# The first norm of a two-layer block: both row tiles of a quarter ahead of the next quarter's modulation copy, and the shift's small operations ahead of the normalised tiles

## The chip, the cores and the metric

The kernel runs on one core of one Trainium2 chip. The metric is the device time of one launch, in microseconds (us). The core has five engines that run side by side, each through its own instructions in order: PE multiplies (its weight loads are shown as PEld), DVE and ACT work on whole tiles element by element, POOL does a little of the same and issues some transfers, SP issues most transfers. A tile lies in on-chip memory on 128 partitions; PE writes its results to eight accumulator banks (PSUM), which DVE and ACT read.

## The reference, cut to what matters

Two layers of a diffusion block over 256 tokens of `x` and 256 of a context `h_ctx`, 1024 wide. Each layer has two gated feed-forward halves around a middle with three branches (neighbourhood attention, window attention, convolution), each behind a normalisation whose scale and shift are products of a conditioning vector. The change touches only the start of the first feed-forward half of the first layer:

```
for l in range(DEPTH):
    mx = split(silu(c) @ w_ada[l] + b_ada[l], 9)       # mx[0] shift, mx[1] scale, mx[2] gate, ...
    mc = split(silu(c_ctx) @ w_ada[l] + b_ada[l], 9)   # the same for the context
    x = x + 0.5*mx[2]*swiglu(rms_norm(x, g[l,0])*(1 + mx[1]) + mx[0], w_ffn1_gu[l], w_ffn1_down[l])
    h_ctx = ...                                        # the same with mc
    ...                                                # middle, second feed-forward half
return rms_norm(x, final_g)

swiglu(h, w_gu, w_down): a, b = split(h @ w_gu); return (silu(a)*b) @ w_down
```

## The kernel before, in words

Activations lie transposed: eight row tiles `R[k]` of 128 features by 512 columns (256 of `x`, then 256 of the context). Every product in full precision is made of three matmuls at reduced precision (`mm3`, L327, L328, L329): high part of the weights by high and by low part of the data, low part by high part. The two parts are made by a split: ACT rounds the value to the high part (L123), DVE subtracts (L124). For weights these are `wh` and `wl`, made from a raw block `raw` that SP's queue brings in (L280); `weights(k)` does it for row tile `k` of the first four weight columns. Four raw buffers form a ring; later in the program the rows of the conditioning's weights (`araw` at L246) go through the same ring.

The opening is `FirstNorm.blocks`. It starts four of the feed-forward's first columns before the norm's root is known: it multiplies the weights by `R[k]` scaled by `modA` (1 + scale, times the norm's weight), and only at the end applies the root `rs` and adds the shift's part. It runs in four quarters `q` of two row tiles each:

- `ada_first(1, q)` makes the scale for the quarter, in two steps of a generator that `go` advances. The first step is 32 small matmuls (L208, into `ada`) and a copy by DVE (L213, `adas`); the second is a transposing matmul (L216, `adat`) and DVE's `mod` (L219), `modt` (L176) and `modA` (L178).
- `scale(k)` makes the two parts of the scaled tile, in two halves each: `qh` on ACT (L521), `ql` on DVE (L522).
- `prod(k)` is 4 columns by 3 matmuls into the four banks `f`.
- `square(k)` is ACT's square (L389) and DVE's sum (L396), for the root.

Behind the quarters comes the shift. The same `ada_first` with chunk 0 makes it (`z[0]` to `z[3]`); `inv_rms` makes `rs` (L370); `parts_of(h)` splits half of the shift (`bb`), `product_of(h)` multiplies it by the four columns' weights (32 matmuls `fb`, L615), `rows_of` copies the row out (`br`, L622) and `fc` (L652) adds the two rows up. For the columns that follow, the normal way is used: `normed(k)` makes `nt` (L469), `hidden` adds the shift and splits into `Hh` (ACT, L494) and `Hl` (DVE, L495). The last two of the eight tiles are normed by POOL (L483), with ACT (L485) and a split. Then the columns `g` run, 8 tiles by 3 matmuls each.

When the feed-forward's first columns are out, `Ada.enter` starts the conditioning for the rest of the block: DVE copies one value into the tile `phase` (L236), POOL issues a transfer of 1 MB into it (L237), ACT takes SiLU of it (L238), and DVE then reduces one row of weights after the other against it (L250). DVE's `fs` (L659) and the gate's products (L725, L727, L730) follow.

The order of the instructions in the opening is the order in which the code is written: `in_order` pins it for each engine from the start of the blocks to `self.end`, and holds the 300 instructions that follow behind them. Behind `self.end`, a scheduler orders them as their inputs allow.

## Time and profile before

| | |
|---|---|
| median of 3 runs | 1979.52 us (1979.29 to 1980.55) |
| profiled execution | 1982.47 us |
| its span | 1980.7 us |
| granted PE clock, mean | 0.994 |
| PE busy | 1947.2 us, 98% of the span |
| DVE / ACT / POOL busy | 71% / 45% / 5% |

The span is the time from the first to the last instruction of the profiled execution. In a row of the timeline stand the start in us, the length, the engine, the line, the operation, the output and its inputs, and how many are taken together; in brackets the idle time before it and what ended it, as far as semaphores show it. A matmul's length is longer than its step: the next one starts before it ends.

### The profile page before, as it was taken

How to read it: one execution, taken by the hardware profiler on the slowest of the kernel's cores; microseconds unless marked ns; L12 is line 12 of the kernel's file. 1: busy time of each engine (PE TensorE's matmuls, PEld its weight loads, DVE VectorE, ACT ScalarE, POOL GpSimd, SP SyncE). 2: the span in 40 equal slices, each digit the busy share in tenths (PEclk: the TensorE clock that was granted, in tenths of full speed). 3: DMA queues.
4: the chain of work that ended last, by engine and by line, in shares of the span. 5: the costliest groups of instructions: out<-in, count | busy, mean ns of one | idle time of the engine just before them, and what ended most of it. 6: DMA issues, size and time to landing. Idle time of an engine off the chain costs nothing.

```text
span 1980.7 us, 29367 instructions
## 1 busy us (share of the span) xinstructions
PE 1947.2 (98%) x10760; PEld 1655.7 (84%) x10760; DVE 1400.4 (71%) x3203; ACT 898.3 (45%) x1765; POOL 106.2 (5%) x100
## 2 busy tenths in 40 slices
PE   6899999999999999999999999999999999999998
PEld 4788888888788888988888888888888988999998
DVE  3698677759867645876666669766665797787654
ACT  3433232344667744533232245323223567866553
POOL 0100000100011101100000010000001001020000
PEclk9899999999999999999999999999999999999999
DMA  8265545523221222354454535444554243355552
GB/s 303 86 227 185 173 152 178 185 76 120 84 75 55 94 97 96 107 172 159 158 160 159 170 107 170 156 154 154 166 170 134 93 146 124 128 179 182 183 185 103
DMA packets 82657, 287.40 MB, mean 145 GB/s; under 512 B 9296, under 2 KB 11088, under 8 KB 82128
## 3 DMA queue, kind: packets, MB, share of 16 engines
q1 hardware_dynamic: 79488, 277.91, 42.9%
q0 software_dynamic: 864, 4.98, 0.6%
q10 hardware_dynamic: 2160, 2.64, 0.5%
q8 instruction: 84, 1.38, 0.3%
q14 instruction: 61, 0.50, 0.1%
HBM read 284.44 MB, written 1.05 MB: 144 GB/s over the span
## 4 chain that ended last, share of the span: by engine, by line
PE 94%; DVE 2%; issue 1%; ACT 1%; DMA 1%; POOL 0%; SPq 0%; ACTq 0%; DVEq 0%; POOLq 0%
PE g L329 13%; PE g L328 13%; PE g L327 13%; PE pr L328 8%; PE pr L327 8%; PE pr L329 8%; PE b L327 4%; PE b L328 4%; PE b L329 4%; PE f L328 3%; PE f L329 3%; PE f L327 3%; PE sc L1050 1%; PE pv L1130 1%; PE pt L1111 1%
## 5 line engine op out<-in xcount | busy, mean ns | idle before, releaser
L123 ACT ACTIVATE wh<-raw 128x512 fp32r<-128x512 f32 x760 | 464.4, 627 | 567.8 <-PE g L328 177.7
L124 DVE TENSOR_TENSOR wl<-raw,wh 128x512 fp32r<-128x512 f32 x760 | 521.6, 696 | 162.1 <-ACT wh L123 157.5
L250 DVE CUSTOM_DVE_ANT_0 junk<-araw,phase 128x512 f32<-128x512 f32 x512 | 353.9, 691 | 235.6 <-DMA araw<-in_adaT_dram 221.7
L329 PE MATMUL g<-Hh,wl 128*128 128x512 f32 (+1 forms) x1240 | 457.8, 369 | 0.0
L327 PE MATMUL g<-Hh,wh 128*128 128x512 f32 (+1 forms) x1240 | 455.2, 367 | 1.8 <-ACT Hh L123 1.8
L328 PE MATMUL g<-Hl,wh 128*128 128x512 f32 (+1 forms) x1240 | 456.8, 369 | 0.0
L327 PEld LDWEIGHTS g<-Hh,wh 128*128 128x128 f32 x1240 | 233.7, 189 | 44.0 <-ACT Hh L123 2.3
L328 PEld LDWEIGHTS g<-Hl,wh 128*128 128x128 f32 x1240 | 234.1, 189 | 42.9 <-DVE Hl L124 0.2
L329 PEld LDWEIGHTS g<-Hh,wl 128*128 128x128 f32 x1240 | 233.6, 188 | 41.3 <-DVE wl L124 0.2
L328 PE MATMUL pr<-gl,wh 128*128 128x512 f32 (+1 forms) x704 | 258.0, 366 | 0.0
L327 PE MATMUL pr<-gh,wh 128*128 128x512 f32 (+1 forms) x704 | 258.0, 366 | 0.0
L329 PE MATMUL pr<-gh,wl 128*128 128x512 f32 (+1 forms) x704 | 257.5, 366 | 0.0
L327 PE MATMUL b<-Hh,wh 128*128 128x512 f32 (+1 forms) x480 | 167.1, 348 | 3.2 <-DVE rot L941 3.2
L328 PE MATMUL b<-Hl,wh 128*128 128x512 f32 (+1 forms) x480 | 163.9, 342 | 0.0
L329 PE MATMUL b<-Hh,wl 128*128 128x512 f32 (+1 forms) x480 | 163.9, 342 | 0.0
L327 PEld LDWEIGHTS pr<-gh,wh 128*128 128x128 f32 x704 | 132.4, 188 | 23.5
L328 PEld LDWEIGHTS pr<-gl,wh 128*128 128x128 f32 x704 | 132.5, 188 | 23.0
L329 PEld LDWEIGHTS pr<-gh,wl 128*128 128x128 f32 x704 | 132.4, 188 | 22.9
L123 ACT ACTIVATE gh<-g 128x512 fp32r<-128x512 f32 (+1 forms) x88 | 50.7, 576 | 218.3 <-DVE g L727 210.1
L328 PE MATMUL f<-ql,wh 128*128 128x258 f32 (+1 forms) x408 | 120.8, 296 | 7.4 <-DVE ql L522 7.4
L327 PE MATMUL f<-qh,wh 128*128 128x258 f32 (+1 forms) x408 | 124.0, 304 | 1.9 <-ACT qh L521 1.6
L329 PE MATMUL f<-qh,wl 128*128 128x258 f32 (+1 forms) x408 | 119.9, 294 | 0.0
(247 smaller groups left out, 2602.6 us busy)
## 6 DMA issues: line engine op xcount, KB each, us to landing
raw<-in_ws_dram SPq DMA_DIRECT2D x380, 512.0 KB, 3.5
araw<-in_adaT_dram SPq DMA_DIRECT2D x128, 512.0 KB, 4.1
araw<-in_ada_dram SPq DMA_DIRECT2D x32, 256.0 KB, 5.7
phase<-in_crow_dram POOLq DMA_DIRECT2D x3, 1024.0 KB, 8.3
tb<-in_rpb_dram ACTq DMA_DIRECT2D x12, 192.0 KB, 2.8
R<-in_xT_dram SPq DMA_DIRECT2D x8, 256.0 KB, 6.0
phase<-in_const_dram POOLq DMA_DIRECT2D x2, 640.0 KB, 6.2
out_dram<-fin SPq DMA_DIRECT2D x4, 256.0 KB, 3.3
```

What stands on the lines that cost most here:

```text
L123: nc.scalar.activation(out=hi, in_=src, func=AF.Copy)
L124: nc.vector.tensor_tensor(out=lo, in0=src, in1=f32(hi), op=ALU.subtract)
L250: nc.vector.tensor_tensor_reduce(out=junk, in0=raw[:, c], in1=self.rows[:, s, c], scale=1.0, scalar=0.0, op0=ALU.mult, op1=ALU.add, accum_ ...
L327: nc.tensor.matmul(ps, wh, xh, start=start, stop=False)
L328: nc.tensor.matmul(ps, wh, xl, start=False, stop=False)
L329: nc.tensor.matmul(ps, wl, xh, start=False, stop=stop)
L1050: nc.tensor.matmul(pss[s][:, o], a[r, c], b[r, k], start=i == 0, stop=i == 2)
L1111: nc.tensor.transpose(pt[:, n * P:(n + 1) * P], self.pf[v][s][:, o + i * P:o + (i + 1) * P], ident)
L1130: nc.tensor.matmul(self.po[s][:, sl], V[t0 + i][j // 2][:, c:c + P], p[:, k], start=m == 0, stop=m == n - 1)
```

## The change

Both halves of the change move code; no instruction is added or taken away. In the quarters, the odd tile's `weights` and `scale` and both squares stand ahead of the first `go(a)` of the next quarter (its matmuls and copy). Three matmuls (one column) of the odd tile stand between that and the second `go(a)`, and nine behind it. `weights(0)` is put between the first quarter's two steps. In the part on the shift, three normed tiles come first, then both remaining modulation groups, the first `fb`, both second steps and the second half's split; only then the early weights, and the other tiles. `hidden` runs for tiles 0 and 1, then 2, then 3 to 5.

```diff
             go(a)
+            weights(0)
             go(a)
             for q in range(4):
                 k = 2 * q
...
-                weights(k)
                 self.scale(k)
+                weights(k + 1)
                 prod(k)
-                if q < 3:
-                    a = ada_first(1, q + 1, raws[q + 1])
-                    go(a)
-                weights(k + 1)
                 self.scale(k + 1)
+                self.square(k, nc.vector)
+                self.square(k + 1, nc.vector)
                 if q == 3:
                     break
-                prod(k + 1, range(2))
+
+                a = ada_first(1, q + 1, raws[q + 1])
                 go(a)
-                prod(k + 1, range(2, n))
-                self.square(k, nc.vector)
-                self.square(k + 1, nc.vector)
+                prod(k + 1, [0])
+                weights(k + 2)
+                go(a)
+                prod(k + 1, range(1, n))
             zero = [ada_load(0, q) for q in range(4)]
             W.load()
             W.load()
-            self.square(KD - 2, nc.vector)
-            self.square(KD - 1, nc.vector)
             norm = inv_rms([self.sq], self.nq, oneD, res)
+            z = [ada_first(0, q, raws) for q, raws in enumerate(zero)]
             prod(KD - 1, [0, 1])
-            z = [ada_first(0, q, raws) for q, raws in enumerate(zero)]
...
             self.rs = res[0]
-            self.H, nts = [], []
+            self.H = []
             prod(KD - 1, [3])
-            go(z[2])
-            product_of(0)
-            nts += [self.normed(k) for k in (0, 1)]
+            nts = [self.normed(k) for k in range(3)]
             go(z[2])
             go(z[3])
-            rows_of(0)
-            nts += [self.normed(k) for k in (2, 3)]
-            self.hidden(range(2), nts)
+            pb = product_of(0)
+            go(z[2])
             go(z[3])
             parts_of(1)
-            product_of(1)
-            self.hidden(range(2, 4), nts)
-            nts += [self.normed(k) for k in range(4, KD - N_POOL)]
-            rows_of(1)
-            self.hidden(range(4, KD - N_POOL), nts)
+            rows_of(pb)
+            pb = product_of(1)
             for _ in range(N_EARLY):
                 W.make()
+            self.hidden(range(2), nts)
+            rows_of(pb)
+            self.hidden([2], nts)
+            nts += [self.normed(k) for k in range(3, KD - N_POOL)]
+            self.hidden(range(3, KD - N_POOL), nts)
             self.end = traced()
             self.hidden(range(KD - N_POOL, KD))
```

`product_of` now returns its bank and `rows_of` takes it. Lines behind the middle of this part stand two lines higher in the new file (L615 becomes L614, L652 becomes L650, L655 becomes L653, L725 becomes L723).

DVE in the second quarter, before (tile 2's `ql` first; `wl` and `ql` behind `adas` are those of the odd tile 3):

```order
L522 SCALAR_TENSOR_TENSOR ql_267<-R_81,modA_104,qh_266 128x256 x2
L213 COPY adas_301<-ada_284 128x128
L124 TENSOR_TENSOR wl_304<-raw_135,wh_303 128x512
L522 SCALAR_TENSOR_TENSOR ql_308<-R_82,modA_104,qh_307 128x256 x2
L219 TENSOR_TENSOR mod_103<-adat_319,vt 128x4
L176 TENSOR_SCALAR modt_322<-mod_103 128x4
L178 TENSOR_TENSOR modA_104<-modt_322,vt 128x4
L396 TENSOR_TENSOR sq_245<-sq_245,sq_331 128x512
L396 TENSOR_TENSOR sq_245<-sq_245,sq_334 128x512
L124 TENSOR_TENSOR wl_338<-raw_172,wh_337 128x512
L522 SCALAR_TENSOR_TENSOR ql_342<-R_83,modA_104,qh_341 128x256 x2
```

and the same piece now:

```order
L522 SCALAR_TENSOR_TENSOR ql_267<-R_81,modA_104,qh_266 128x256 x2
L124 TENSOR_TENSOR wl_273<-raw_135,wh_272 128x512
L522 SCALAR_TENSOR_TENSOR ql_289<-R_82,modA_104,qh_288 128x256 x2
L396 TENSOR_TENSOR sq_208<-sq_208,sq_294 128x512
L396 TENSOR_TENSOR sq_208<-sq_208,sq_297 128x512
L213 COPY adas_317<-ada_300 128x128
L124 TENSOR_TENSOR wl_323<-raw_176,wh_322 128x512
L219 TENSOR_TENSOR mod_103<-adat_326,vt 128x4
L176 TENSOR_SCALAR modt_329<-mod_103 128x4
L178 TENSOR_TENSOR modA_104<-modt_329,vt 128x4
L522 SCALAR_TENSOR_TENSOR ql_342<-R_83,modA_104,qh_341 128x256 x2
```

The odd tile's `wl` and `ql` and both sums of squares went ahead of the copy `adas`; behind it stands the next quarter's `wl`.

DVE in the part on the shift, before, from the copy of `z[2]` to the second half's `bb`:

```order
L213 COPY adas_579<-ada_562 128x128
L469 SCALAR_TENSOR_TENSOR nt_614<-R_79,modA_104,rs_557 128x256 x2
L469 SCALAR_TENSOR_TENSOR nt_617<-R_80,modA_104,rs_557 128x256 x2
L219 TENSOR_TENSOR mod_103<-adat_620,vt 128x4
L213 COPY adas_640<-ada_623 128x128
L622 COPY br_642<-fb_581 4x512
L469 SCALAR_TENSOR_TENSOR nt_644<-R_81,modA_104,rs_557 128x256 x2
L469 SCALAR_TENSOR_TENSOR nt_647<-R_82,modA_104,rs_557 128x256 x2
L495 SCALAR_TENSOR_TENSOR Hl_651<-nt_614,mod_103,Hh_650 128x256 x2
L495 SCALAR_TENSOR_TENSOR Hl_657<-nt_617,mod_103,Hh_656 128x256 x2
L219 TENSOR_TENSOR mod_103<-adat_662,vt 128x4
L124 TENSOR_TENSOR bb<-mod_103,bb 128x4x2
```

and now, from the first normed tile to the first `Hl`:

```order
L469 SCALAR_TENSOR_TENSOR nt_562<-R_79,modA_104,rs_557 128x256 x2
L469 SCALAR_TENSOR_TENSOR nt_565<-R_80,modA_104,rs_557 128x256 x2
L469 SCALAR_TENSOR_TENSOR nt_568<-R_81,modA_104,rs_557 128x256 x2
L213 COPY adas_588<-ada_571 128x128
L213 COPY adas_607<-ada_590 128x128
L219 TENSOR_TENSOR mod_103<-adat_642,vt 128x4
L219 TENSOR_TENSOR mod_103<-adat_645,vt 128x4
L124 TENSOR_TENSOR bb<-mod_103,bb 128x4x2
L621 COPY br_650<-fb_609 4x512
L124 TENSOR_TENSOR wl_686<-raw_482,wh_685 128x512
L124 TENSOR_TENSOR wl_690<-raw_482,wh_689 128x512
L495 SCALAR_TENSOR_TENSOR Hl_694<-nt_562,mod_103,Hh_693 128x256 x2
```

Both copies, both `mod` and the split of the second half went ahead of every `Hl` and of the fourth normed tile.

ACT behind the pinned part, before, at the last hidden tile (`nt_750` is the tile that POOL normed, `Hh_748` its high part):

```order
L485 ACTIVATE nt_750<-nt_750,mod_103,modA_104 128x256 x2
L238 ACT_TABLE_LOAD
L238 ACTIVATE phase_775<-phase_775 128x2048
L123 ACTIVATE Hh_748<-nt_750 128x512
L123 ACTIVATE wh_961<-raw_959 128x512
```

and now:

```order
L485 ACTIVATE nt_750<-nt_750,mod_103,modA_104 128x256 x2
L123 ACTIVATE Hh_748<-nt_750 128x512
L238 ACT_TABLE_LOAD
L238 ACTIVATE phase_775<-phase_775 128x2048
L723 ACTIVATE g_781<-fs_767,sb_765 128x256 x2
```

The scheduler put `Hh` of the last tile ahead of the load of SiLU's table and of the SiLU itself.

More of the change, by code (lines that the diff above doesn't have):

```diff
@@ L603, in blocks @@
             bb = cpool.tile([P, KD, 4], F32R, name="bb")
-            pbs, brs = [], []
+            brs = []
             def parts_of(h):
@@ L617, in product_of, with rows_of @@
                                 start=k == 4 * h and j == 0, stop=k == 4 * h + 3 and j == 1)
-                pbs.append(pb)
-            def rows_of(h):
+                return pb
+            def rows_of(pb):
                 br = S(name="br")
-                nc.vector.tensor_copy(br[:4, :n * P], pbs[h][:4, :n * P])
+                nc.vector.tensor_copy(br[:4, :n * P], pb[:4, :n * P])
                 brs.append(br)
```

## The prediction

> **What bounds the kernel now.** I read the page first, then busy time by stretch of the opening, then the waits there, then the timeline. The page's row of busy time, and behind it the stretches (columns: stretch, length, busy time and count of PE, PEld, DVE, ACT, POOL, granted clock, DMA share, GB/s):
>
> ```profile
> PE 1947.2 (98%) x10760; PEld 1655.7 (84%) x10760; DVE 1400.4 (71%) x3203; ACT 898.3 (45%) x1765; POOL 106.2 (5%) x100
> ```
>
> ```profile
> 25.90:36.60 10.70, 7.87 (x59) 5.40 (x58) 4.87 (x12) 3.79 (x8) 0.00 (x0) 1.00 1.06 394
> 36.60:48.60 12.00, 9.16 (x65) 6.52 (x64) 7.56 (x17) 4.55 (x8) 0.00 (x0) 1.00 0.39 139
> 48.60:69.50 20.90, 16.17 (x233) 13.86 (x232) 13.82 (x42) 8.30 (x21) 1.27 (x1) 0.84 0.01 1
> 69.50:87.30 17.80, 15.97 (x57) 12.21 (x57) 9.42 (x19) 10.48 (x17) 3.84 (x2) 0.82 0.47 178
> ...
> 110.00:390.00 280.00, 280.00 (x1207) 226.32 (x1206) 216.28 (x534) 87.23 (x159) 7.65 (x6) 1.00 0.55 182
> ```
>
> PE is the bound, and from 110 us it has no gap: 280.00 / 1207 = 0.232 us a matmul. Anything it idles in the opening is therefore paid in full, and the change touches nothing else. One quarter of the opening, from its modulation's matmuls (L208) on:
>
> ```profile
> 25.96 1.08 PE L208 MATMUL ada<-araw,cs 128*32 128x128 f32 x32
> 27.11 0.29 DVE L213 COPY adas<-ada 128x128 f32<-128x128 f32 x1 [3.94 <-PE ada L208]
> 27.32 0.68 DVE L124 TENSOR_TENSOR wl<-raw,wh 128x512 fp32r<-128x512 f32 x1
> 27.92 0.87 DVE L522 SCALAR_TENSOR_TENSOR ql<-R,modA,qh 128x256 fp32r<-128x256 f32 x2
> 28.85 0.50 PE L328 MATMUL f<-ql,wh 128*128 128x512 f32 x1 [1.38 <-DVE ql L522]
> 30.12 0.28 PE L216 MATMUL adat<-sel,adas 128*128 128x4 f32 x2
> 31.04 0.91 ACT L521 ACTIVATE qh<-R,modA 128x256 fp32r<-128x256 f32 x2 [6.04 <-DVE modA L178]
> 33.85 0.50 PE L328 MATMUL f<-ql,wh 128*128 128x512 f32 x1 [1.34 <-DVE ql L522]
> 36.61 1.08 PE L208 MATMUL ada<-araw,cs 128*32 128x128 f32 x32
> 48.65 1.08 PE L208 MATMUL ada<-araw,cs 128*32 128x128 f32 x32
> ```
>
> PE waits twice: at 28.85, because DVE had sat 3.94 us behind the copy `adas` and only then made `wl` and `ql` of the odd tile; at 33.85, because only six matmuls (1.4 us) stand between the transposing matmul `adat` and the next tile, whose chain mod, modA, qh, ql takes longer.
>
> **Part A, the quarters.** After the change `scale` and `weights` of the odd tile no longer follow the copy, so the first wait goes; three matmuls (0.70 us) stand over the copy (it ends at 27.40, 1.44 us after the group's start at 25.96, of which the group takes 1.08) and nine (2.1 us) behind `adat`. From `adat` (30.12) it is 0.92 to the first `qh` (31.04); its first half is done 0.5 later, and `ql`'s two halves (0.87) at about 32.5: 2.4 us. `adat` (0.2), the nine matmuls and the next tile's first (0.23) make 2.5. So the second wait closes too, by 0.1 us. A quarter then holds 24 matmuls of 0.232 (5.57), the modulation's 1.08 and `adat`'s 0.2, 6.8 us; with 0.2 for restarts, whose first row is longer (0.50), 7.0. The last stretch, to the first modulation of the shift, holds 30 matmuls: 8.4. Before, the modulation groups begin at 16.12, 25.96, 36.61 and 48.65:
>
> ```profile
> 16.12 1.08 PE L208 MATMUL ada<-araw,cs 128*32 128x128 f32 x32
> ```
>
> 32.5 us against 7.0 + 7.0 + 8.4 = 22.4: 10.1 gained. DVE's own work of a quarter (4.87 us from 25.9 to 36.6, and nothing is added) and ACT's (3.79) fit into 7.0. The start loses some: `weights(0)` now stands ahead of the second `go(a)`.
>
> ```profile
> 8.63 0.63 ACT L123 ACTIVATE wh<-raw 128x512 fp32r<-128x512 f32 x1 [4.65 <-DMA raw<-in_ws_dram]
> 9.04 0.16 DVE L219 TENSOR_TENSOR mod<-adat,vt 128x4 f32<-128x4 f32 x1 [0.68 <-PE adat L216]
> 10.60 0.80 PE L327 MATMUL f<-qh,wh 128*128 128x512 f32 x1 [1.60 <-ACT qh L521]
> ```
>
> `wl` can begin at 9.3 (wh's end) and takes 0.7, so mod goes from 9.04 to about 10.0, and PE's start by 0.9. The tile's twelve matmuls fill 10.60 to 16.12, 0.46 each; where full speed comes at a time and not after a count, the last two of them run at 0.23 after the change, and 0.4 returns: I take 0.5 (0 to 0.9, by whether all or nothing returns). A = 10.1 − 0.5 = **9.6** (8.5 to 10.4; the low end if each quarter still waits 0.3 us for ql).
>
> **Part B, the shift to the first hidden tiles.**
>
> ```profile
> 53.96 0.60 ACT L370 ACTIVATE rs<-rstd 128x512 f32<-128x512 f32 x1 [0.56 <-PE rstd L368]
> 54.55 1.08 PE L208 MATMUL ada<-araw,cs 128*32 128x128 f32 x32
> 54.63 1.27 POOL L483 TENSOR_TENSOR nt<-R,rs 128x512 f32<-128x512 f32 x1 [53.59 <-ACT rs L370]
> 55.91 1.67 DVE L469 SCALAR_TENSOR_TENSOR nt<-R,modA,rs 128x256 f32<-128x256 f32 x4
> 57.74 1.08 PE L208 MATMUL ada<-araw,cs 128*32 128x128 f32 x32
> 62.86 0.14 DVE L219 TENSOR_TENSOR mod<-adat,vt 128x4 f32<-128x4 f32 x1
> 63.59 0.26 PE L615 MATMUL fb<-wh,bb 128*4 128x128 f32 x1 [3.97 <-DVE bb L124]
> 67.20 0.68 DVE L622 COPY br<-fb 4x512 f32<-4x512 f32 x1 [0.26 <-PE fb L615]
> 69.58 0.49 PE L327 MATMUL g<-Hh,wh 128*128 128x512 f32 x1
> 84.02 0.88 PE L327 MATMUL g<-Hh,wh 128*128 128x512 f32 x2 [1.82 <-ACT Hh L123]
> 87.26 0.63 PE L327 MATMUL g<-Hh,wh 128*128 128x512 f32 x1
> ```
>
> The last `mod` stands behind four normed tiles and two `Hl` on DVE, and PE waits 3.97 us. What follows keeps the clock of before (part A's gain is not taken off). After the change three normed tiles (6 × 0.42) end at 57.1, both `adas` copies at 57.7; PE does the two modulation groups back to back (54.55 to 56.6), then the first `fb` and the `adat`, which between 55.6 and 57.74 took 2.2 us, to 58.8; two mod and the two parts of bb take some 1.1 (62.86 to 63.59 is 0.7 with one mod), to 59.9; the second `fb` at the first one's pace ends at 61.9. The first `g` follows at about 62.4, since nearly all of `fc` is put behind the fourth `g`. But the `Hl` chain is DVE's: br 0.6, two wl 1.2, Hl 0 and 1 (four halves, at `nt`'s 1.67 for four), br 0.6, Hl 2 (0.83), nt 3 to 5 (2.5), Hl 3 to 5 (2.5) is 9.9 us from 59.9, to 69.8. PE does nine `g` matmuls by 65.5, waits there, and goes on unbroken from the `Hl` of tile 5 at about 69.7. The `g` matmul that begins at 87.26 before has 54 `g` matmuls ahead of it in both orders; 37 of them then remain, 8.6 us: 78.3. The last hidden tile is not late: its normed tile comes from POOL (3.12 us from about 70.8), ACT takes some 1.6 for scale, shift and split (`qh`'s 0.91 and `wh`'s 0.63), so it is ready at 75.5, which is when the 26th of the 37 wants it (69.7 + 25 × 0.232), and its `Hh` no longer stands behind the SiLU that waits for the phase's transfer (the 1.82 us above). B = 87.3 − 78.3 = **8.9** (7.3 to 9.4).
>
> **Part C, what is late next.** The reductions L250 free the ring's raw buffers, and wait for SiLU, and it for the phase's transfer:
>
> ```profile
> 71.11 0.72 POOL L237 DMA_DIRECT2D phase<-in_crow_dram  x1 [15.21 <-DVE phase L236]
> 71.85 3.12 POOL L483 TENSOR_TENSOR nt<-R,rs 128x512 f32<-128x512 f32 x1
> 80.24 1.28 ACT L238 ACT_TABLE_LOAD   x1 [3.58 <-DMA phase<-in_crow_dram]
> 83.48 0.69 DVE L250 CUSTOM_DVE_ANT_0 junk<-araw,phase 128x512 f32<-128x512 f32 x1 [7.00 <-ACT phase L238]
> 84.70 2.48 DVE L659 TENSOR_TENSOR fs<-f,rs 128x512 f32<-128x512 f32 x4
> 106.26 1.16 ACT L123 ACTIVATE wh<-raw 128x512 fp32r<-128x512 f32 x2 [2.58 <-DMA raw<-in_ws_dram]
> 108.46 0.39 PE L327 MATMUL g<-Hh,wh 128*128 128x512 f32 x1
> ```
>
> The copy L236 comes about 1 us earlier, and `fs` (2.48) and the last `Hl` (0.6) now fall ahead of the first L250 rather than into their row; with some 1.6 of DVE's idle time ahead of it (an estimate from the 7.00 shown) the reductions move 5.7 us where PE moves 8.9. The weights made at 106.26 are for the column that begins at 108.46, 1.5 us after its first `wh`; so PE waits about 3.2 − 1.5 = 1.7 there, once (0 to 2.5). Clock:
>
> ```profile
> 81.03:84.44 3.41, 1.58 (x7) 0.96 (x7) 0.96 (x3) 3.40 (x5) 0.00 (x0) 1.00 0.04 17
> 84.44:87.85 3.41, 3.41 (x10) 2.59 (x9) 3.41 (x7) 1.48 (x4) 0.00 (x0) 0.50 0.00 0
> ```
>
> After 3.41 us with 1.58 busy the next 3.41 ran at 0.50. PE's new wait at 65.5 to 69.7 can bring one such window: 1.6 us lost, of which the wait for the ring takes the same time back. So the two are one term, **−1.7** (0 to −4). The Trainium skill, "TensorE: Matmul & The Clock Gate", section "HAM oscillation — how this bites in real kernels", lets the clock fall only after an idle gap of some 3.4 us; by it no window would be lost. The trace here differs: 0.50 followed a window that was busy for 1.58 of its 3.41 us, so idle for no more than 1.83, and the measurement decides.
>
> **Sum.** 9.6 + 8.9 − 1.7 = 16.8. The profiled execution took 1982.47 (span 1980.7), giving 1965.7; the median of the runs, 1979.52, is 2.95 below it, giving **1962.7**. Ends: 8.5 + 7.3 − 4 = 11.8, so 1967.7; 10.4 + 9.4 = 19.8, so 1959.7.
>
> **Rivals.**
> - POOL and DVE collide at `rs`. POOL's first normed tile (54.63) took 1.27 us with DVE idle until 55.70; now both start on `rs`. The row at 71.85 took 3.12 beside a busy DVE, so POOL yields; if DVE yields, its chain is up to 1.3 us later: 1964.0. The Trainium skill, "SBUF — State Buffer", section "SBUF: two separate sides", says of the shared ports that whichever starts first holds them for the whole instruction, which would give this case; the trace shows POOL stretched and no DVE row lengthened.
> - The `Hl` chain is slower, and a half-rate window falls on it: half of B is left, 1967.2.
> - Neither ring nor clock costs anything: 1961.0.
> - Transfers hold the quarters. The second quarter runs at DMA share 1.06; were the tiles late, half of A would go: 1967.5. Against it: no wait above is for `R` or `araw`, and after 36.6 the share is 0.39.
> - Slower: the raw ring falls behind for good, and PE waits for weights in each of the 20 pairs of columns that follow. At 0.84 us a pair the 16.8 are gone; from 1.04 on the kernel is over 0.2% slower (1983.5). Against it: 216.28 of 280 us DVE, so slack returns in each column.
>
> **Chances.** Forecast 0.55 (its own range 1961.5 to 1964); collision 0.13; half of B 0.12; neither cost 0.13; transfers 0.03; slower 0.02; some gain under 0.2% 0.02, where ring and clock together take most of it. What a measurement can tell from no change is about 0.2%, 4 us. Range 1959.7 to 1967.7; faster 0.96, same 0.02, slower 0.02.
>
> **Signs.** L208 groups 7 us apart, the first of the next chunk at about 39 (A); the waits for `ql` of 1.3 us gone; second `fb` not waiting 3.97; `Hh` of the last tile ahead of the table load, no PE wait of 1.8 for it; one PE wait for `wh` some 38 us behind the first `g` (C). Wrong would be: PE waits for `ql` that remain, a stall in more than one column, half-rate windows at other places.

## The result, and the profile after

The changed kernel takes 1966.95 us (median of 6 runs, 1966.14 to 1968.24) against 1979.72 (6 runs of before beside it, 1979.29 to 1982.26): ratio 0.9934, with an interval of 0.9921 to 0.9947, so 12.8 us less. In a later pair of runs it was 1967.24 against 1978.46, ratio 0.9940 (0.9926 to 0.9953), 11.2 us less. The forecast was 1962.7 with a range of 1959.7 to 1967.7: the direction and the range hold, the point is 4.25 us too low, and the time lies outside the 1961.5 to 1964 that the forecast gave as its own. The profiled execution took 1967.16 us, so against the profiled one of before (1982.47) it is 15.3 less, where the sum said 16.8.

The page's span and busy row, and then the opening by stretches (columns as in the prediction: stretch, length, busy time and count of PE, PEld, DVE, ACT, POOL, granted clock, DMA share, GB/s):

```profile
span 1965.4 us, 29367 instructions
...
PE 1941.9 (99%) x10760; PEld 1650.6 (84%) x10760; DVE 1402.2 (71%) x3203; ACT 897.6 (46%) x1765; POOL 107.5 (5%) x100
```

```profile
16.40:23.40 7.00, 7.00 (x59) 5.43 (x58) 4.90 (x12) 3.80 (x8) 0.00 (x0) 1.00 1.04 402
23.40:30.40 7.00, 7.00 (x59) 5.40 (x58) 5.04 (x13) 3.80 (x8) 0.00 (x0) 1.00 1.05 396
30.40:38.80 8.40, 8.40 (x65) 6.56 (x64) 5.20 (x13) 4.56 (x8) 0.00 (x0) 1.00 1.05 401
38.80:52.40 13.60, 12.80 (x219) 10.73 (x218) 8.85 (x26) 3.92 (x11) 1.28 (x1) 1.00 0.13 52
52.40:69.80 17.40, 15.32 (x69) 11.55 (x70) 14.36 (x32) 12.67 (x23) 5.03 (x2) 1.00 0.48 182
69.80:110.00 40.20, 40.20 (x174) 32.49 (x173) 36.57 (x91) 17.04 (x32) 0.00 (x0) 1.00 0.53 172
```

The instruction count is that of a reordering: PE's 10760 and DVE's 3203 are the same as before. PE is busy through all three quarters, where one quarter of before had 7.87 of 10.70 and the next 9.16 of 12.00. The shift keeps about 2.9 us of PE's idle time (0.8 and 2.1), and from 69.8 on there is none. The clock of the two stretches on the shift is 1.00; it was 0.84 and 0.82.

The timeline of the same execution, at the places that answer to the rows of before:

```profile
11.11 0.80 PE L327 MATMUL f<-qh,wh 128*128 128x512 f32 x1 [2.86 <-ACT qh L521]
16.48 1.08 PE L208 MATMUL ada<-araw,cs 128*32 128x128 f32 x32
23.48 1.08 PE L208 MATMUL ada<-araw,cs 128*32 128x128 f32 x32
30.46 1.08 PE L208 MATMUL ada<-araw,cs 128*32 128x128 f32 x32
38.86 1.08 PE L208 MATMUL ada<-araw,cs 128*32 128x128 f32 x32
44.81 3.59 DVE L469 SCALAR_TENSOR_TENSOR nt<-R,modA,rs 128x256 f32<-128x256 f32 x6 [0.99 <-ACT rs L370]
44.86 1.28 POOL L483 TENSOR_TENSOR nt<-R,rs 128x512 f32<-128x512 f32 x1 [43.81 <-ACT rs L370]
50.12 0.22 PE L614 MATMUL fb<-wh,bb 128*4 128x128 f32 x1 [0.79 <-DVE bb L124]
57.95 0.50 PE L328 MATMUL g<-Hl,wh 128*128 128x512 f32 x1 [0.64 <-DVE Hl L495]
60.67 4.31 POOL L483 TENSOR_TENSOR nt<-R,rs 128x512 f32<-128x512 f32 x1
61.35 2.48 DVE L124 TENSOR_TENSOR wl<-raw,wh 128x512 fp32r<-128x512 f32 x4
66.14 0.63 ACT L123 ACTIVATE Hh<-nt 128x512 fp32r<-128x512 f32 x1
66.79 1.28 ACT L238 ACT_TABLE_LOAD   x1
66.83 0.97 PE L327 MATMUL g<-Hh,wh 128*128 128x512 f32 x3 [1.07 <-ACT Hh L123]
69.81 0.40 PE L327 MATMUL g<-Hh,wh 128*128 128x512 f32 x1
87.74 1.15 ACT L123 ACTIVATE wh<-raw 128x512 fp32r<-128x512 f32 x2 [1.79 <-DMA raw<-in_ws_dram]
```

The four groups on L208 stand 7.00, 6.98 and 8.40 us apart. The second `fb` waits 0.79 instead of 3.97. The last tile's `Hh` is ahead of the table load, but PE still waits 1.07 for it. At 69.81 begins the matmul with 54 `g` matmuls ahead of it that stood at 87.26: 17.45 us earlier.

Two numbers are used for every profile below. **z** is the start of the shift's first L208 group (48.65 before, 38.86 after): what the quarters gain is seen in it. **S** is the stretch from z to that 55th `g` matmul (38.61 before, 30.95 after): what the shift gains is seen in it. The last column is the time in which the granted clock was at half between 20 and 110 us.

| run | edit | median us | before beside it | ratio and interval | z | S | half rate, us |
|---|---|---|---|---|---|---|---|
| before | | 1979.72 | | | 48.65 | 38.61 | 13.7 |
| after | | 1966.95 | 1979.72 | 0.9934 (0.9921 to 0.9947) | 38.86 | 30.95 | 0 |
| before_again | before, unchanged | 1977.77 | 1977.14 | 1.0002 (0.9992 to 1.0012) | 48.03 | 35.04 | 6.8 |
| quarters_only | new quarters, old shift | 1969.6 | 1977.14 | 0.9961 (0.9949 to 0.9973) | 38.74 | 35.10 | 6.8 |
| shift_only | old quarters, new shift | 1974.53 | 1977.14 | 0.9989 (0.9980 to 0.9998) | 47.31 | 30.98 | 3.4 |
| w0_late | after, `weights(0)` later | 1966.19 | 1977.14 | 0.9947 (0.9932 to 0.9961) | 37.83 | 30.96 | 3.4 |
| pool_early | after, POOL's tiles early | 1966.29 | 1979.84 | 0.9933 (0.9908 to 0.9958) | 38.17 | 32.61 | 6.8 |
| rs_copy | after, POOL has its own `rs` | 1964.38, one run | 1979.84 | | 37.73 | 30.83 | 3.4 |
| phase_late | after, phase's copy later | 1971.65, one run | 1979.84 | | 38.35 | 31.14 | 3.4 |
| before_filled | before, 17 matmuls more | 1979.51, one run | 1979.84 | | 48.19 | 34.87 | 3.4 |
| after_again | after, unchanged | 1967.24 | 1978.46 | 0.9940 (0.9926 to 0.9953) | 37.82 | 30.95 | 3.4 |
| combo2 | after, three edits | 1966.07 | 1978.46 | 0.9934 (0.9922 to 0.9947) | 37.36 | 32.75 | 6.8 |
| cover_six | after, six matmuls ahead | 1969.62, one run | 1978.46 | | 40.52 | 31.59 | 6.8 |
| nts_late | after, normed tiles later | 1967.37, one run | 1978.46 | | 38.13 | 33.81 | 6.8 |

Rows with the same number for before beside them belong to one group of runs. Times are to be compared within a group; across groups, only ratios. Where one run is given there is no interval, and its time alone shows little; its profile is what is read.

### The profile page after: what moved, and what is told of

It is laid out like the page before. It is cut to its first block, busy times and chain, and to the rows that moved or that the text cites. A ratio compares the mean times of both kernels' runs of the same rounds, so it can differ in the third digit from the quotient of the medians.

```text
span 1965.4 us, 29367 instructions
## 1 busy us (share of the span) xinstructions
PE 1941.9 (99%) x10760; PEld 1650.6 (84%) x10760; DVE 1402.2 (71%) x3203; ACT 897.6 (46%) x1765; POOL 107.5 (5%) x100
## 3 DMA queue, kind: packets, MB, share of 16 engines
HBM read 284.44 MB, written 1.05 MB: 145 GB/s over the span
## 4 chain that ended last, share of the span: by engine, by line
PE 94%; DVE 2%; ACT 1%; issue 1%; DMA 1%; POOL 0%; SPq 0%; ACTq 0%; POOLq 0%; DVEq 0%
PE g L327 13%; PE g L329 13%; PE g L328 13%; PE pr L327 8%; PE pr L328 8%; PE pr L329 8%; PE b L327 4%; PE b L329 4%; PE b L328 4%; PE f L327 3%; PE f L328 3%; PE f L329 3%; PE sc L1048 1%; PE pv L1128 1%; PE pt L1109 1%
## 5 line engine op out<-in xcount | busy, mean ns | idle before, releaser
L250 DVE CUSTOM_DVE_ANT_0 junk<-araw,phase 128x512 f32<-128x512 f32 x512 | 353.7, 691 | 225.0 <-DMA araw<-in_adaT_dram 218.1
```

Source lines behind the costliest of these rows:

```text
L250: nc.vector.tensor_tensor_reduce(out=junk, in0=raw[:, c], in1=self.rows[:, s, c], scale=1.0, scalar=0.0, op0=ALU.mult, op1=ALU.add, accum_ ...
```

## Experiments

### The kernel before, profiled a second time

The question was whether the terms of the sum, all from one profiled execution, are those of a usual run. No edit. Expected:

> The kernel before, unchanged, for a second profile. The profiled run shown so far took 1982.47 us, 2.75 above its median; the changed kernel's profiled run stood 0.2 above its own. Theory 1 (the excess is pace: matmul steps some 0.2% longer over the whole program): the opening ends as before, first g at 69.6 us within 0.5, and three half-rate windows between 60 and 88. Theory 2 (the excess is clock windows of the opening that a median run does not have): first g between 66.5 and 68.5, or the matmul that began at 87.26 now 1.5 to 3 earlier, with one or two half-rate windows fewer.

The timeline of this second profile, at the shift's first group and the 55th `g` matmul, and ACT's row for the phase:

```profile
48.03 1.08 PE L208 MATMUL ada<-araw,cs 128*32 128x128 f32 x32
77.16 1.28 ACT L238 ACT_TABLE_LOAD   x1 [1.20 <-DMA phase<-in_crow_dram]
83.07 0.39 PE L327 MATMUL g<-Hh,wh 128*128 128x512 f32 x1
```

S is 35.04, not 38.61. Most of the difference, 3.57 us, follows from one transfer. The tile `phase` by itself, time from issue to landing, in the first profile of before and then in the second:

```profile
DMA to landing us min/median/max: 9.1/9.1/9.1
```

```profile
DMA to landing us min/median/max: 6.8/6.8/6.8
```

In the first profile it landed 2.3 us later behind its issue; SiLU, and behind it on ACT the last tile's `Hh`, were late, PE waited the 1.82 us that the prediction quotes, and a half-rate window followed. In that window the `g` matmuls come 0.43 us apart instead of 0.23, some 1.3 us up to the row at 87.26. Neither is in the second profile. Theory 2 was the nearer one, but the 55th `g` matmul comes 4.19 us earlier, more than its 1.5 to 3, and what it names, clock windows, is only a part of it. Two other profiles with the old shift (quarters_only 35.10, before_filled 34.87) agree with the second.

### Each part alone

The quarters with the old shift, and the shift with the old quarters: each file takes one part of the diff and leaves the other as it was.

> The quarters of the changed kernel with the shift part of before. Theory 1 (the two parts are separate terms): modulation groups 7.0, 7.0 and 8.4 apart, first group of the shift at 38.9, first g at 69.6 - 9.8 = 59.8, time 9 to 10 us under before. Theory 2 (the parts are not separate: clock windows of the shift stage move with it): the same to 38.9, then first g off by more than 1.5 from 59.8, gain under 8 or over 11.5.

> The quarters of before with the shift part of the changed kernel. Theory 1: first group of the shift at 48.65 as before, first g 7.35 earlier than before (62.2), the third column's third tile 7.7 earlier, no half-rate window after the shift, time 7 to 8 us under before. Theory 2 (part of the gain was given back later, by the raw ring or by pace): the same opening, time only 3 to 5 us under before, since 12.8 in all was measured and 9.8 would be the quarters'.

By timing the quarters alone give 7.7 us (0.9961), the shift alone 2.2 (0.9989): 9.9 together, against 11.2 to 12.8 for both at once, which the intervals do not tell apart. Both gains are below what theory 1 expected (9 to 10, and 7 to 8), the shift's also below theory 2 (3 to 5). In the profiles the parts are separate: quarters_only has z of after (38.74) and S of before_again (35.10 against 35.04), shift_only a z near that of before (47.31) and S of after (30.98). The first group of the shift and the 55th `g` matmul, in quarters_only and then in shift_only:

```profile
38.74 1.08 PE L208 MATMUL ada<-araw,cs 128*32 128x128 f32 x32
73.84 0.40 PE L327 MATMUL g<-Hh,wh 128*128 128x512 f32 x1
```

```profile
47.31 1.08 PE L208 MATMUL ada<-araw,cs 128*32 128x128 f32 x32
78.29 0.39 PE L327 MATMUL g<-Hh,wh 128*128 128x512 f32 x1
```

So neither part needs the other, and S of the new shift is 4.1 us below the usual S of the old one. That the expected time of shift_only came from the first profile of before, whose S is 38.61, is most of its miss.

### The start: `weights(0)`

```diff
             go(a)
-            weights(0)
             go(a)
+            weights(0)
```

> The changed kernel with weights(0) behind the second step of the first modulation, as in before. Theory (moving it ahead cost the start): mod at 9.0 or earlier, first f at 10.6 instead of 11.1, second modulation group at 16.12 instead of 16.48, everything behind it 0.3 to 0.5 us earlier, time the same within what can be measured. Rival (full speed comes after a count of work, not at a time): the second group comes 0.9 earlier or not at all.

From ACT's first `wh` to PE's first `f` it is 2.00 us here (8.91 to 10.91), 2.82 in after (8.29 to 11.11) and 1.97 before (8.63 to 10.60). So `weights(0)` ahead of the second step costs 0.8 us at the start, as reckoned (0.9). But z is at 37.83 here and at 37.82 in after_again, which has `weights(0)` early. Two things that the kernels have in common scatter by as much as the effect. ACT's first `wh`, which waits for the first weight block, begins between 7.79 us (after_again) and 8.91 (here). And the first tile's matmuls go from 0.43 to 0.23 us a step at some 14.2 us here and 14.5 in after_again, but at 16.2 in after. From the first `f` that is 3.3, 3.9 and 5.1 us, so full speed does not come after a fixed count of work. The timing (0.9947) lies with that of after; a gain from this edit cannot be separated.

### POOL and DVE at `rs`

The rival in the prediction had POOL and DVE colliding where both start on `rs`, with DVE giving way. Two kernels: POOL reads a copy of `rs` made by ACT, or POOL makes both of its tiles early and so occupies that place for longer.

```diff
             self.rs = res[0]
+            self.rsp = S(name="rsp")
+            nc.scalar.activation(out=self.rsp[:, :NT], in_=self.rs[:, :NT], func=AF.Copy)
...
-    nc.gpsimd.tensor_tensor(out=t[:, full], in0=R[k][:, full], in1=self.rs[:, full], op=ALU.mult)
+    nc.gpsimd.tensor_tensor(out=t[:, full], in0=R[k][:, full], in1=self.rsp[:, full], op=ALU.mult)
```

> The changed kernel with a copy of rs for POOL, made by ACT 0.6 us behind rs, so that DVE starts its first normed tile ahead of POOL. Theory (whichever starts first keeps the other out): DVE's first product 0.47 us instead of 1.60, POOL's stretched until DVE's run of six ends (over 2 us instead of 1.28); second fb at the same place, 11.26 us behind the first modulation group within 0.2, since PE's own row of groups, fb and adat ends there. Rival (the 1.13 us are on the path): second fb 0.6 to 1.1 earlier. Second rival (no lock, the row is only long): DVE's first product stays at 1.6.

```diff
             self.hidden(range(3, KD - N_POOL), nts)
+            for k in range(KD - N_POOL, KD):      # both of POOL's tiles, used by hidden below
+                t = self.pooled[k] = S(name="nt")
+                nc.gpsimd.tensor_tensor(out=t[:, :NT], in0=R[k][:, :NT], in1=self.rs[:, :NT], op=ALU.mult)
             self.end = traced()
```

> The changed kernel with both of POOL's normed tiles issued behind one another, ahead of the phase's transfer. Theory (the last hidden tile is late because POOL's second product, released at 60 us, waits 3 us for DVE to fall idle): no wait of PE for the last Hh (1.07 in the changed kernel), the stretch from the first modulation group of the shift to the third column's third tile 29.6 us instead of 30.95, time 1.3 us lower, which the runs cannot separate. Rival (POOL's second product now takes the port from DVE in front of the last mod and bb): second fb starts 0.5 to 1.3 later than 11.26 us behind that group, and nothing is won.

The line of `nt` on DVE by itself, between 43 and 52 us (columns: durations in ns as minimum, median, maximum, then first and last start), in after and then in rs_copy:

```profile
L469 DVE SCALAR_TENSOR_TENSOR nt<-R,modA,rs x6: 472/474/1605, 44.8 to 47.9; 128x256 f32<-128x256 f32 x6
```

```profile
L469 DVE SCALAR_TENSOR_TENSOR nt<-R,modA,rs x6: 472/476/1501, 43.7 to 46.7; 128x256 f32<-128x256 f32 x6
```

The timeline of rs_copy at the same place:

```profile
43.67 3.49 DVE L469 SCALAR_TENSOR_TENSOR nt<-R,modA,rs 128x256 f32<-128x256 f32 x6 [0.99 <-ACT rs L370]
44.38 1.31 POOL L483 TENSOR_TENSOR nt<-R,rsp 128x512 f32<-128x512 f32 x1 [43.34 <-ACT rsp L628]
48.88 0.22 PE L614 MATMUL fb<-wh,bb 128*4 128x128 f32 x1 [0.79 <-DVE bb L124]
```

In after five of DVE's six operations take 0.47 us and one takes 1.60: DVE gives way, as the rival said. The copy moves the collision, and does not remove it: POOL starts 0.7 us later, inside DVE's run, and one later DVE operation takes 1.50. POOL keeps its 1.31 us; that it would be held up until DVE's run of six ends, as expected, did not come. So shared data is not the cause, and being first does not protect DVE. One such step does not cost the 1.3 us of the rival: in after the second `fb` comes 11.26 behind z, in rs_copy 11.15. PE's own row (the modulation's matmuls, then the first `fb` to 48.7) ends about when DVE's delayed one does (both copies done at 48.8), which the forecast for the rival had not counted. No run is free of the collision, so its small price is read from these rows and not shown by a run. In pool_early two POOL operations (2.69 us) cost DVE two such steps, six operations 4.61, and there the second `fb` does come 1.0 us later, 12.27 behind z, as that run's rival said.

### What holds the stretch: the last hidden tile

In pool_early PE's wait for the last `Hh` is gone, since POOL no longer makes the tile late, and yet S is 32.61, longer than in after, because two half-rate windows fall into it. combo2 puts three edits together: `weights(0)` late, POOL's tiles early, and only two normed tiles ahead of the modulation with the third behind the second `rows_of`.

> The changed kernel with three edits: weights(0) behind the first modulation's second step, POOL's two normed tiles issued together ahead of the phase's transfer, and two normed tiles instead of three on DVE ahead of the shift's small operations, so that the copies are not late behind POOL's second product. Theory: first f 0.8 earlier, no wait of PE for adat over 0.4 and none for the last Hh, the stretch from the first modulation group of the shift to the third column's third tile 29.4 without a half-rate window (30.95 in the changed kernel); time 1.5 to 2.5 us under the changed kernel of the same chip. Rival (waits taken from PE come back as half-rate windows, as in the run with both of POOL's tiles early): that stretch 31 to 33, and a time like the changed kernel's.

It takes 12.4 us off (0.9934), after on the same chip 11.2 (0.9940): nothing that the intervals tell apart, so no version that surely beats after was found. S is 32.75, as its rival said. What the stretch hangs on can be read from all the profiles together. Where POOL makes its second tile late (after, after_again, w0_late, shift_only), the last `Hh` on ACT begins 27.28, 27.29, 27.30 and 27.30 us behind z, and S is 30.95, 30.95, 30.96 and 30.98, though one half-rate window lies in three of them and none in after. One window costs nothing there: PE then waits less for that `Hh`, as in after_again:

```profile
65.79 0.97 PE L327 MATMUL g<-Hh,wh 128*128 128x512 f32 x3 [0.29 <-ACT Hh L123]
```

rs_copy (27.17, one window, S 30.83) agrees. Two windows are more than the wait hides: cover_six below has the last `Hh` at 27.28 too, PE waits for none, and S is 31.59. Where the tile is early (pool_early, combo2, and phase_late below) PE waits for no `Hh`, and the windows are paid: a whole one holds 8 matmuls at 0.427 instead of 0.232 us and so loses 1.56. With two of them S is 32.61 and 32.75, with one 31.14. In pool_early and phase_late another 1.0 comes from the collision, since PE's `adat` waits 1.03 for the late `adas`; in combo2 PE waits 1.03 for an `Hl` instead. So the late tile costs after the 1.07 us of PE's wait at most, and no profile without it was free of half-rate windows; whether that us can be had was not shown.

### The normed tiles behind the products

```diff
             prod(KD - 1, [3])
-            nts = [self.normed(k) for k in range(3)]
             go(z[2])
...
             pb = product_of(1)
+            nts = [self.normed(k) for k in range(3)]
```

> The changed kernel with the three normed tiles behind the shift's small operations instead of ahead of them. Theory (the hidden chain on DVE sets the pace from the shift on, and DVE's 2.5 us of normed tiles were free where PE ran groups and the first fb): second fb no earlier than 10.8 us behind the shift's first group (11.26 in the changed kernel), the stretch to the third column's third tile 2 to 3 us longer than 30.95. Rival (what counts is when the second fb runs): that stretch the same or shorter.

PE's row for the first low part in this kernel:

```profile
54.04 0.50 PE L328 MATMUL g<-Hl,wh 128*128 128x512 f32 x1 [2.04 <-DVE Hl L495]
```

The second `fb` comes at z + 11.04, only 0.2 earlier than in after, PE waits 2.04 for the first `Hl`, and S is 33.81, 2.9 longer. Of this 2.2 is the chain: the last `Hh`, behind DVE's work and POOL's tile, begins 29.45 behind z instead of 27.28. The other 0.7 goes with the two half-rate windows of this run, as in cover_six. The three early tiles are what DVE can do while PE makes the modulation; put later, they lengthen the chain that PE waits for. The single time, 1967.37, does not show it: its later part is shorter than after's by about 2 us, of which 1.5 is one place in the middle of the first layer (650 to 680 us) that is taken up below.

### The clock in the stretch before

```diff
                 pb = PS("fb")
+                if h:
+                    for i in range(17):
+                        nc.tensor.matmul(pb, wts[0][0][0], self.Q[0][0][:, :NT], start=True, stop=True)
```

Seventeen matmuls of 128x512 stand in before ahead of the second `fb`, where PE waits; what they write is overwritten by `fb`.

> The kernel before with 17 matmuls of 128x512 (4 us) that feed nothing in front of the second fb, where PE waits 4.0 us for bb; their sums are overwritten. They keep PE busy and leave every other engine as it is. Theory 1 (the hidden chain on DVE sets when the g columns can run, the clock there costs little): no half-rate window at the second fb, the stretch from the first modulation group of the shift to the third column's third tile 34.5 to 35.1, as in the second profile of before (35.04). Theory 2 (the windows are the cost): 31.5 to 33.5.

PE's granted clock around that place, windows of one length, in before_again (without the extra matmuls) and then in before_filled:

```profile
56.37:59.79 3.42, 2.23 (x48) 1.85 (x44) 2.26 (x7) 1.14 (x3) 0.00 (x0) 1.00 0.00 0
59.79:63.20 3.41, 0.22 (x4) 0.25 (x5) 2.90 (x10) 0.78 (x3) 0.00 (x0) 1.00 0.00 0
63.20:66.61 3.41, 3.41 (x33) 3.19 (x30) 3.33 (x9) 2.46 (x7) 0.00 (x0) 0.51 0.00 0
66.61:70.03 3.42, 3.12 (x21) 2.69 (x21) 3.42 (x10) 3.42 (x8) 0.00 (x0) 0.99 0.01 2
70.03:73.44 3.41, 3.41 (x10) 2.69 (x9) 2.98 (x5) 1.53 (x3) 3.10 (x2) 0.51 0.70 231
```

```profile
59.55:62.96 3.41, 3.41 (x16) 2.64 (x14) 3.13 (x10) 0.38 (x2) 0.00 (x0) 1.00 0.00 0
62.96:66.37 3.41, 2.51 (x36) 2.21 (x34) 3.18 (x9) 2.46 (x7) 0.00 (x0) 1.00 0.00 0
```

With PE kept busy the half-rate window at the second `fb` is gone, and S is 34.87 against 35.04: the same. There the clock costs nothing, and DVE's chain of normed and hidden tiles sets the pace, as the working of the shift assumed.

### How many matmuls stand over the copy

```diff
-                prod(k + 1, [0])
+                prod(k + 1, [0, 1])
                 weights(k + 2)
                 go(a)
-                prod(k + 1, range(1, n))
+                prod(k + 1, range(2, n))
```

> The changed kernel with six matmuls instead of nine behind each quarter's transposing matmul (two columns of the odd tile in front of it, two behind). Theory (nine cover the chain mod, modA, qh, ql of 2.4 us by 0.1; six are 0.7 short): a wait of PE for ql of 0.5 to 0.7 in each of three quarters, groups 7.6 to 7.7 apart instead of 7.0, the shift's first group 1.7 to 2.1 later. Rival (only the odd tile's place mattered): groups 7.0 apart.

The groups stand at 16.19, 23.83, 31.47 and 40.52, so 7.64, 7.64 and 9.05 apart: 1.95 us more over three quarters than in after. Its waits between 16 and 41 us (engine, tile, line, what it waited for; total, times, longest):

```profile
PEld f L327 <- ACT qh L521: 1.6, 3, 0.5
...
PEld f L328 <- DVE ql L522: 1.0, 3, 0.3
```

With six matmuls left behind `adat` instead of nine the wait for the scaled tile comes back, 0.5 us for `qh` and 0.3 for `ql` in each quarter. Nine just cover that chain.

### The ring of raw buffers

```diff
         if ada_end:
-            ada.enter(mod[l][:, 3 * br * KD, 0:1])
+            ada.enter(pend[0][0][0][:, 0:1] if isinstance(norm, FirstNorm) else mod[l][:, 3 * br * KD, 0:1])
```

The copy into `phase` takes a value of the first `fs` instead of one of the shift, so it cannot start earlier; the transfer overwrites it.

> The changed kernel with the copy that releases the phase's transfer made to depend on the first fs, so that it comes 6 to 10 us later on DVE; POOL's second product moves ahead of the transfer. Theory of part C (phase, SiLU, reductions and ring are one chain, with some 2 us of slack): first reduction later by as much, and PE waits for weights about 38 us behind the first g, 4 to 8 us in all. Rival (the ring has other slack): no wait of PE over 0.5 us between the opening and 130 us.

DVE's and PE's rows of phase_late:

```profile
66.89 0.14 DVE L236 COPY phase<-fs 128x1 f32<-128x1 f32 x1
75.74 0.69 DVE L250 CUSTOM_DVE_ANT_0 junk<-araw,phase 128x512 f32<-128x512 f32 x1 [1.35 <-ACT phase L238]
92.74 0.50 PE L327 MATMUL g<-Hh,wh 128*128 128x512 f32 x1 [1.69 <-ACT wh L123]
```

The first L250 is 5.7 us later than in after (70.04), and PE waits 1.69 us for weights 17 us further on. The wait lies between theory (4 to 8 us) and rival (none over 0.5). So the chain that the prediction described (copy, transfer, SiLU, reduction, raw buffer, weights) is real, but after had slack in it, and does not wait. The run is 4.7 us longer than after: PE's matmuls, 0.3 us ahead of after's at 90 us, are 1.6 behind at 110, this wait; another 1.9 is lost between 670 and 680, where PE waits 0.48 and 1.09 for `pf` (1.09 once in after) and a half-rate window follows; and 1.2 near 1660, where a half-rate stretch lasts 6.83 us and in after 3.41.

### The changed kernel again

> The changed kernel, unchanged, beside the kernel before on the same chip. Theory (the removed waits are worth 9 to 11 us in every run, and the rest of the gain is how many half-rate windows a run of either kernel draws): 10 to 13.5 us under before; the stretch from the first modulation group of the shift to the third column's third tile 30.95 within 0.3, with one window or none. Rival (the opening's 13.3 to 17.5 us are kept): 13.5 or more under before.

S is 30.95 once more, z is 37.82 instead of 38.86 (the first `f` is 0.5 us earlier, and full speed comes at 14.5 instead of 16.2), and one half-rate window lies at 55.5 to 58.9, which after did not have. The time is the same: the 1.04 us are lost again near 1655, where the half-rate stretch lasts 6.83 us and in after 3.41.

## Why the prediction was right, and where its point was off

**Part A held.** The quarters were to take 7.0 + 7.0 + 8.4 = 22.4 us; the groups stand 7.00, 6.98 and 8.40 apart, 22.38. The wait for `ql` closes by as little as reckoned: cover_six, with three matmuls less behind `adat`, has it back. z moved 9.79 us against 9.6, and against the second profile of before 9.17; `weights(0)` costs 0.8 at the start, and the half of it that was to come back cannot be told from the scatter of the first transfer and of the time at which full speed comes (16.2 us in both profiles of the pair, 14.2 to 15.9 in the other runs with the new quarters).

**Part B: the steps held, its size did not.** Second `fb` at 50.1 by the working (59.9 less A's 9.8), 50.12 in the trace; first `g` at 52.6, measured 52.44; and by 59.9 PE has begun 18 `g` matmuls, where the working has 17. Of the wait that it puts ahead of that, only 0.64 us came (57.95): `fc` and the wait for its `br` fill 2.0 us, where the working leaves some 1.0 (65.5 less 62.4 less nine matmuls). The term was 8.9 us. The profile pair shows 7.66, and against the second profile of before 4.09. Two steps of it failed:

- "the median of the runs, 1979.52, is 2.95 below it, giving **1962.7**." Durations came from one execution, and its excess over the median was taken off the time but left in the terms. That excess lay in the very stretch: its late transfer, the wait of 1.82 us and the window behind it make 3.1 of the 3.57 us that separate S of the two profiles. B counted their removal as a gain, and a usual run of before does not have them to lose. 8.9 − 3.57 leaves 5.3.
- "The last hidden tile is not late: its normed tile comes from POOL (3.12 us from about 70.8)". POOL took 4.31, waiting until DVE's run of `wl` subtractions ended at 63.83 and ending 1.15 later; the tile was ready 1.1 us too late, and PE waits 1.07 for its `Hh`. That is most of the 1.2 between 5.3 and the measured 4.1.

**Part C: the chain of the ring is real, but nothing was lost to it; the window came by another way.** The forecast had 1.7 us lost, to the ring and to one half-rate window. The ring costs nothing in after: the reductions moved 16.4 us (their second row from 87.88 to 71.45) where PE moved 17.45, so they fell behind by 1 us, not by the 3.2 reckoned, and the slack of some 1.5 holds that. (From before_again they moved 13.4, and PE 13.3.) phase_late shows the wait that a later phase brings. The reason that they moved so far is the transfer again: it landed 4.8 us behind its issue in after and 9.1 before. A half-rate window at the place of the new wait (65.5 to 69.7 in before's clock, so 55.7 to 59.9 after) is there in after_again (55.5 to 58.9) and in w0_late, and is hidden by the late last tile; in the profile of after it did not come at all. But the wait did not bring it: it follows a window with `fc` in which PE was busy for 3.05 of 3.41 us and waited no longer than 0.37.

**What is given back later.** The 17.45 us of the opening become 15.3 at the end of the profile pair. Against before_again the opening shows 13.26 and the end 10.9, near what timing says (11.2 to 12.8). So "Anything it idles in the opening is therefore paid in full" was off by about 2.2 us: they are given back behind the opening, where all engines have the same instructions in the same order (DVE from 148 us on). The starts of PE's matmuls, compared one by one, show where. Between 650 and 680 us before_again loses 1.2 of its distance from after, the first profile of before 1.5: PE's wait in the middle of the first layer, in after and then in before_again:

```profile
671.84 0.94 PE L1109 MATMUL pt<-ident,pf 128*128 128x128 f32 x4 [1.09 <-ACT pf L1093]
```

```profile
684.14 0.95 PE L1111 MATMUL pt<-ident,pf 128*128 128x128 f32 x4 [0.62 <-ACT pf L1095]
```

ACT waits there for a later transfer into `phase`, 2.7 us in after and 1.6 in before_again. It landed 7.3 us behind its issue in after, 6.2 in before_again, and 5.8 in the first profile of before, where PE's wait is 0.3. Another 2.0 us go between 680 and 1400, spread, with no wait of PE; and 1.1 come back near 1660, where the half-rate stretch lasts 3.41 us in after and 6.83 in both profiles of before. Why the transfer lands later, and what is lost up to 1400, stays open; in combo2, pool_early and rs_copy the sum of it all is smaller or absent.

Put together, the point is 4.25 us low: 1.5 because the profile pair shows 15.3 for 16.8, and 2.95 because the profiled execution of before stood that far above its median, less the 0.2 by which that of after stands above its own. With 5.3 for B the same sum, taken from the median, is 1966.3, close to the time. In part that is luck: C's 1.7 was not lost where it was forecast, while 1.07 for the last `Hh` and about 2 us behind the opening were lost that no term had. **Rivals:** the collision at `rs` happened as told and cost next to nothing; half of B is left against a usual run, and the time that this rival gave (1967.2) is the nearest, but it came through the profile chosen, not a slower `Hl` chain; neither ring nor clock cost anything in the profile of after, but the 1961.0 of that rival did not follow; no transfer held the quarters (DMA share 1.05, PE unbroken); the slower case did not come, the ring having slack from the first column on.

## What to carry to other kernels

Before a wait is counted as a gain, look at it in a second profile of the same kernel: if the profiled execution stands above the median, its excess lies in some stretch, and it may be the one that is to be improved. To cover a fixed chain of small operations, count the large ones that stand over it: 9 matmuls of 0.232 us covered 2.4 us of chain, and 6 brought back 0.6 us a quarter. When one wait is taken away from a stretch, ask at once what is the next to be late there; here it was one tile by POOL, and a half-rate window hid behind it.

## What the runs showed of the hardware

- **The half-rate windows last 3.41 us or twice that, on a grid whose phase differs from run to run; in the opening they follow a window in which PE did little or ran the tiny `fc` matmuls.** In before_again the window at 59.79 has PE busy for 0.22 us, and the next is at 0.51; the one at 66.61 is busy for 3.12 us, but with the tiny `fc` matmuls, and the next is at 0.51 too. The same instructions gave no half-rate window in this stretch in after and one in after_again, where PE was busy for 3.05 us of the window before. The Trainium skill, "TensorE: Matmul & The Clock Gate", section "HAM oscillation — how this bites in real kernels", wants an idle gap of some 3.4 us; here a window that is mostly busy with small matmuls was enough, and the measurement decides. In pool_early two half-rate windows follow each other though PE was busy throughout the first; why is open:

```profile
52.19:55.60 3.41, 3.04 (x24) 2.42 (x21) 3.41 (x9) 1.46 (x5) 0.00 (x0) 1.00 0.54 159
55.60:59.01 3.41, 3.41 (x12) 2.82 (x12) 3.41 (x10) 3.41 (x9) 0.00 (x0) 0.50 0.00 0
59.01:62.43 3.42, 3.42 (x10) 2.65 (x9) 3.10 (x9) 3.42 (x7) 0.72 (x1) 0.50 0.15 38
62.43:65.84 3.41, 3.41 (x16) 2.80 (x15) 3.41 (x7) 1.92 (x5) 0.00 (x0) 1.00 0.94 357
```

- **These windows go with the spread of a kernel's runs.** Unchanged before ranged from 1974.45 to 1983.92 us on one chip, and its runs sort by granted clock: 1974.5 to 1976.6 at 0.997, 1976.7 to 1978.8 at 0.996, 1977.4 to 1982.1 at 0.995, 1979.1 to 1983.9 at 0.994. On the chip of after_again they hardly do (1976.7 to 1980.2 at 0.996, 1977.1 to 1979.4 at 0.995), so the windows are not the whole spread. A step of 0.001 is 3.95 us at half rate, 1.8 us by the matmuls' pace (1.56 for 3.41).
- **POOL and DVE hinder each other in both directions.** Beside DVE's three-operand operations on `nt` POOL keeps its 1.3 us, and one DVE operation takes 1.5 to 1.6 us instead of 0.47. Beside a run of DVE's two-operand subtractions POOL waits to the end of the run (4.31 us, and 3.12 before). The Trainium skill, "SBUF — State Buffer", section "SBUF: two separate sides", has whichever starts first keep the shared ports for its whole instruction; the stretched DVE operation of rs_copy, which begins 0.09 us behind POOL's, fits that; that of after begins 0.05 us ahead of POOL's by the trace and does not; POOL's wait over several separate DVE instructions goes further than that.
- **The 1 MB transfer into `phase`** took 9.1 us from issue to landing in the first profile of before; 3.1 of the 3.57 us by which S is longer there follow from it. With the old shift it otherwise took 6.4 to 6.8 us (three profiles), with the new one 4.7 to 5.5 (nine profiles; 6.4 in phase_late). So it is not scatter alone; why the new order lands it sooner was not tested.
